# Pairs of column chunks of a feed-forward's first matrix multiplied as seven block products instead of eight, with the matrix pieces queued by due time and x kept in DRAM meanwhile

## The chip, the cores and the metric

The program runs on one core of one Trainium2 chip. The core's engines are TensorE (PE in the profile, with its weight loads as PEld), VectorE (DVE), ScalarE (ACT), GpSimd (POOL) and SyncE (SP), which here issues the DMAs. The metric is the device time of one execution in microseconds (us), the median of several runs; lower is better. Before the change it is 1352.48 us, the median of three runs (1351.2 to 1352.58).

## The reference

The model has two layers. Each is a feed-forward sub-layer, a token mixer and a second feed-forward sub-layer, on 256 tokens of 1024 channels in float32. The change touches only the four feed-forward sub-layers, and in them only the product with the first matrix:

```python
def swiglu_ffn(h, w_in, w_out):                 # w_in: 1024 x 5632, w_out: 2816 x 1024
    gate, up = jnp.split(h @ w_in, 2, axis=-1)
    return (jax.nn.silu(gate) * up) @ w_out

for i in range(DEPTH):                          # DEPTH = 2
    f = swiglu_ffn(rmsnorm(x, ffn1_norm_pre[i]), ffn1_w_in[i], ffn1_w_out[i])
    x = x + 0.5 * rmsnorm(f, ffn1_norm_post[i])
    ...                                         # the token mixer
    f = swiglu_ffn(rmsnorm(x, ffn2_norm_pre[i]), ffn2_w_in[i], ffn2_w_out[i])
    x = x + 0.5 * rmsnorm(f, ffn2_norm_post[i])
```

## The kernel before

**How a float32 product is made.** Every operand of a large product is split in two: a part `hi`, the value rounded to TensorE's one-pass float32 format (`F32R`), and a part `lo`, the value less `hi`. A product is three matmuls that add up in PSUM: hi by hi, hi by lo, lo by hi (`mm3`, L588). The activations are split once for each sub-layer, into `xt`. The matrices come from DRAM as pieces of 128 partitions x 1024 elements, 512 KB each, and each piece is split on the chip: ScalarE casts `whi<-raw` (128x1024), and then VectorE, or GpSimd in some places of the mixer, subtracts `wlo<-raw,whi`.

**The first product of a feed-forward.** `w_in` is laid out as 11 chunks of 512 columns, 256 of the gate and 256 of the matching up columns. One chunk is four pieces; each holds two blocks of 128 rows of the 1024 rows by the 512 columns. `proj_in` (L594) goes over the chunks. For each it multiplies both blocks of 128 tokens (`tb` 0 and 1) by every piece, 12 matmuls of 512 columns for a piece and 48 for a chunk, and `ev` turns the sums in PSUM into gated values: ScalarE takes Silu of the first 256 columns (`ag<-mm,rstd`), VectorE multiplies by the other 256 (`ag<-mm,rstd,ag`). `fin` transposes the gated values in small blocks on VectorE (`way<-ag`), sends them through DRAM to finish the transposition (the DMAs `way<-way`), and splits the outcome for the second product: ScalarE casts `act<-way`, GpSimd subtracts `act<-way,act` (128x512). The second product (`proj_out`, 22 pieces of `w_out`) reads `act`; `post` then adds to `x`.

**What sets the order.** PE executes in the order in which the program is written. The class `Stream` (L243) runs the pieces: `load` issues a piece's DMA and its two splitting instructions whenever PE is done with a piece. There are four buffers for `raw` and `RING = 8` for `whi` and for `wlo`, so splits can be at most eight pieces ahead of PE. In a feed-forward every `wlo` is on VectorE (the list `side` is False there). `Lanes` issues the smaller jobs (the transposed activations, the steps of `fin`) at counted ticks of PE's program. In the profile nearly all instructions stand at the lines of helpers: L144 and L150 for PE, L124 for VectorE and GpSimd, L171 for ScalarE, so they are told apart by the names of what they write and read.

## Time and profile before

| | |
|---|---|
| span of the profiled execution | 1349.7 us |
| median of the three runs | 1352.48 us |
| PE busy | 1327.1 us, 98% of the span |
| VectorE busy | 933.8 us, 69% |
| ScalarE busy | 732.3 us, 54% |
| GpSimd busy | 445.5 us, 33% |
| mean granted TensorE clock | 0.999 of full speed |

The profile is of one execution; its span, from the first to the last instruction, is 1349.7 us. What lies around the span is not in the profile: the median of the runs is 2.8 us more. Matmuls are pipelined, so the duration of one matmul in the profile is about twice the distance from one to the next, and "PE busy" is an upper bound. The share of an engine is a mean over stages that differ: in the chain of waits the long stretches of PE in the four feed-forwards begin at 14, 506, 688 and 1175 us and last 158 to 169 us each; the mixers lie between the first and the second, and between the third and the fourth. In an idle time, the name after the arrow is what ended it.

### The profile page before, as it was taken

The numbers are of one execution on the slowest core, as the hardware profiler recorded it, in microseconds if no ns is written. First come the engines' busy times: TensorE is split into PE (matmuls) and PEld (weight loads), VectorE is DVE, ScalarE is ACT, GpSimd is POOL, SyncE is SP. The second block draws the span as 40 slices with busy tenths as digits, with TensorE's granted clock in tenths as the row PEclk, the third lists the DMA queues.
The fourth block names the chain that finished last, engine by engine and source line by source line (L and its number), as shares of the span: only waits on it lengthen the run. The fifth ranks groups of instructions, "written<-read, shape, count | busy, mean of one in ns | idle before, by whom it ended". The sixth has DMA issues, their size and how long they took to land.

```text
span 1349.7 us, 20220 instructions
## 1 busy us (share of the span) xinstructions
PE 1327.1 (98%) x7259; PEld 1128.0 (84%) x7259; DVE 933.8 (69%) x1594; ACT 732.3 (54%) x1175; POOL 445.5 (33%) x374
## 2 busy tenths in 40 slices
PE   9999999999999999999999999999999999999998
PEld 7888889997787888888888888899977878888886
DVE  6676455999966776665576654579999666766553
ACT  7545447675555545544455543577656564555541
POOL 0111017798744201111011120277986431011110
PEclk9999999999999999999999999999999999999999
DMA  8878746562634666776468775465545446477861
GB/s 274 287 239 260 249 156 210 166 211 96 206 110 153 225 218 222 276 249 221 155 219 280 265 235 186 146 231 172 173 138 183 143 139 234 154 261 247 273 212 39
DMA packets 115652, 273.76 MB, mean 203 GB/s; under 512 B 24768, under 2 KB 48352, under 8 KB 115552
## 3 DMA queue, kind: packets, MB, share of 16 engines
q1 hardware_dynamic: 115264, 272.40, 61.5%
q8 instruction: 57, 0.93, 0.3%
q14 instruction: 43, 0.35, 0.1%
q10 hardware_dynamic: 288, 0.07, 0.0%
HBM read 256.68 MB, written 15.75 MB: 202 GB/s over the span
## 4 chain that ended last, share of the span: by engine, by line
PE 81%; DVE 11%; ACT 3%; DMA 2%; issue 1%; POOL 1%; DVEq 0%; POOLq 0%; SPq 0%; ACTq 0%
PE mm L144 75%; DVE cacc L124 4%; PE gd L144 3%; DVE c L124 3%; DVE wlo L124 2%; PE tr L150 2%; DMA raw<-mw 2%; ACT whi L171 1%; DVE at L124 1%; ACT dt L171 1%; ACT sg L171 0%; DMA raw<-w2i 0%; DVE ssk L124 0%; DVE qk L124 0%; POOL rk L124 0%
## 5 line engine op out<-in xcount | busy, mean ns | idle before, releaser
L144 PE MATMUL mm<-whi,xt 128*128 128x512 f32 (+1 forms) x2048 | 647.6, 391 | 3.0 <-ACT qT L171 2.2
L171 ACT CAST whi<-raw 128x1024 fp32r<-128x1024 f32 (+2 forms) x448 | 458.8, 1035 | 316.8 <-PE mm L144 173.8
L124 DVE TENSOR_TENSOR wlo<-raw,whi 128x1024 fp32r<-128x1024 f32 (+2 forms) x342 | 427.2, 1264 | 190.0 <-ACT whi L171 183.5
L144 PEld LDWEIGHTS mm<-whi,xt 128*128 128x128 f32 x2048 | 382.3, 188 | 82.3 <-ACT qT L171 3.0
L144 PE MATMUL mm<-wlo,xt 128*128 128x512 f32 (+1 forms) x1024 | 396.4, 387 | 0.1
L124 POOL TENSOR_TENSOR wlo<-raw,whi 128x1024 fp32r<-128x1024 f32 (+1 forms) x106 | 250.5, 2379 | 142.5 <-ACT whi L171 140.0
L144 PEld LDWEIGHTS mm<-wlo,xt 128*128 128x128 f32 x1024 | 192.6, 188 | 37.6 <-DVE wlo L124 1.3
L144 PE MATMUL mm<-whi,act 128*128 128x512 f32 x704 | 218.3, 390 | 0.0
L124 POOL TENSOR_TENSOR act<-way,act 128x512 fp32r<-128x512 f32 x44 | 79.1, 1798 | 396.1 <-ACT act L171 385.9
L124 DVE SCALAR_TENSOR_TENSOR cacc<-hT,pc,cacc 128x254 f32<-128x254 f32 (+28 forms) x464 | 179.5, 472 | 0.2
L144 PE MATMUL mm<-xt,whi 128*128 128x256 f32 x960 | 175.5, 285 | 0.8 <-ACT qT L171 0.6
L144 PEld LDWEIGHTS mm<-whi,act 128*128 128x128 f32 x704 | 132.2, 188 | 27.4
L144 PEld LDWEIGHTS mm<-xt,whi 128*128 128x128 f32 x960 | 149.4, 192 | 1.9 <-ACT qT L171 0.9
L144 PE MATMUL mm<-wlo,act 128*128 128x512 f32 x352 | 137.0, 389 | 0.0
L144 PE MATMUL mm<-xt,wlo 128*128 128x256 f32 x480 | 135.9, 283 | 0.0
L171 ACT ACTIVATE ag<-mm,rstd 128x256 f32<-128x256 f32 x88 | 41.7, 474 | 100.0 <-PE mm L144 80.5
L144 PEld LDWEIGHTS mm<-xt,wlo 128*128 128x128 f32 x480 | 92.0, 192 | 0.0
L124 DVE SCALAR_TENSOR_TENSOR ag<-mm,rstd,ag 128x256 f32<-128x256 f32 x88 | 42.3, 481 | 58.7 <-ACT ag L171 58.4
L144 PEld LDWEIGHTS mm<-wlo,act 128*128 128x128 f32 x352 | 66.1, 188 | 13.6
L124 POOL TENSOR_TENSOR rpost<-ss,exp 128x1 f32<-128x1 f32 x12 | 6.5, 538 | 193.8 <-DVE ss L124 193.8
L171 ACT ACTIVATE jk<-mm 128x512 f32<-128x512 f32 x24 | 14.3, 598 | 60.4 <-PE mm L144 60.4
L124 DVE SCALAR_TENSOR_TENSOR c<-mm,pc,c 128x255 f32<-128x255 f32 (+2 forms) x108 | 43.7, 478 | 2.6 <-ACT c L171 2.6
(187 smaller groups left out, 1148.3 us busy)
## 6 DMA issues: line engine op xcount, KB each, us to landing
raw<-mw SPq DMA_DIRECT2D x168, 512.0 KB, 3.8
raw<-w2i SPq DMA_DIRECT2D x88, 512.0 KB, 4.8
raw<-w1i SPq DMA_DIRECT2D x84, 512.0 KB, 4.9
raw<-w1o SPq DMA_DIRECT2D x44, 512.0 KB, 4.7
raw<-w2o SPq DMA_DIRECT2D x44, 512.0 KB, 4.3
way<-way SPq DMA_DIRECT2D x176, 64.0 KB, 1.8
way<-way SPq DMA_DIRECT2D x44, 256.0 KB, 4.8
wbc<-feat SPq DMA_DIRECT2D x13, 512.0 KB, 4.9
```

Of the source, the lines that this page charges most:

```text
L124: r = op(out, *a, **k)
L144: r = self.eng.matmul(o, w, x, **k)
L150: r = self.eng.transpose(*a)
L171: r = op(*a, **k)
```

## The change

Two consecutive chunks make a unit: the 1024 rows and the 1024 columns of the two chunks are seen as a matrix of 2 x 2 blocks of 512 rows and 512 columns, and the activations as 2 x 2 blocks of 128 tokens and 512 channels. The unit's product of two 2 x 2 block matrices is computed from seven block products instead of eight (the Winograd form of Strassen's algorithm). Chunks 6, 7 and 9, 10 of the first feed-forward and 3, 4, 6, 7 and 9, 10 of the other three are units, 11 in all; the other chunks stay as they were. The parts:

- `unit` does seven products of 12 matmuls, 84 where two chunks had 96. Three intermediate sums are copied from PSUM by ScalarE (`kept`), and three of the four results are finished by an addition on VectorE (`gate`, `ag<-mm,sm`, 128x512) ahead of Silu and the multiplication, both then on values in SBUF.
- A unit needs seven matrix forms of two pieces each: three blocks as they are (named 11, 21, 22) and four sums (t1 to t4). So 14 pieces are cast and subtracted where there were eight, and eight more 128x1024 subtractions make the sums, in place in the tiles that hold the raw pieces. Those tiles stay occupied longer; besides the four `raw` buffers they are free slots of the activations (`held`) and the two tiles of `x` (`x0`, `x1`).
- For this, `x` is written to DRAM when the sub-layer begins (`spill`; in the very first it is there already) and read back during the second product (`back`).
- `early` makes the four sums of activation blocks (`xs`) once for each sub-layer, on VectorE and ScalarE.
- From `early` to the end of the first product the pieces are no longer split as they come: `Stream.plan` and what it calls place casts, subtractions and sums on ScalarE, VectorE and GpSimd by planned times and by when PE needs each piece, `bring` issues the DMAs, and `in_order` fixes the order on the three engines as planned. GpSimd takes weight subtractions and sums there, and the subtraction `act<-way,act` moves from GpSimd to VectorE.

```diff
+UNITS = ({6: {"11": (8, 9), "12": ("x0", "x1"), "22": (7, 13), "21": (10, 17)},
+          9: {"11": (9, 10), "12": ("x0", "x1"), "21": (13, 17)}},) + 3 * (
+    {3: {"11": (5, 6), "12": (7, 8), "22": (9, None), "21": (10, 17)}, 6: {"11": (8, 9), "12": ("x0", "x1"), "22": (None, 13), "21": (10, 17)},
+     9: {"11": (9, 10), "12": ("x0", "x1"), "21": (13, 17)}},)
...
+FORMS = ("11", "t1", "t2", "21", "t3", "22", "t4")
+SUMS = {"t1": ("12", "12", "11"), "t2": ("12", "22", "12"), "t3": ("11", "12", "11"), "t4": ("21", "21", "12")}
...
 class Stream:
...
+    def bring(self, now):
+        while self.raws:
+            raw = self.raws[0]
...
+            if self.fetch > now + CFG["depth"]:
+                break
+            self.raws.pop(0)
+            raw.tile = self.fresh() if raw.key is None else self.held(raw.key)
+            self.nc.sync.dma_start(raw.tile[:, :raw.src.shape[-1]], raw.src)
...
+    def best(self, eng, now, until, ahead):
...
+        at, mine = max(eng.at, now), max(self.vec.at, now)
+        for p in self.pieces[self.taken:self.nload + ahead]:
+            kind, t = self.jobs(p)
+            dead = due
+            due += p.use
...
+            if eng is self.gp:
+                mine = max(mine, t) + 1.17
+                if t + 2.4 > max(mine, dead - (CFG["slack"] if kind == "low" else CFG["sums"])):
+                    continue
...
+    def issue(self, eng, t, p, kind):
...
+        if kind == "sum":
+            a, b = (r.tile for r in p.ins)
...
+                eng.tensor_tensor(p.raw.tile, a, b, op=ALU.subtract)
...
+        elif kind == "high":
+            self.to_high(p, slice(0, n))
...
+            self.to_low(p, slice(0, n), eng)
...
     def ffn(xt, l, units, wpost, after, first=2, tails=None):
...
-                    W.tensor_tensor(lo, src, hi.bitcast(F32), op=ALU.subtract)
+                        V.tensor_tensor(lo, src, hi.bitcast(F32), op=ALU.subtract)
...
+        def early():
...
+            def whole(o, r, h):
+                t = blk[r, h].bitcast(F32)
+                V.tensor_tensor(o, t[:, 0], t[:, 1], op=ALU.add)
...
+            def high(n, src):
+                S.copy(sums[n][:, 0], src)
...
+            def low(n, src):
+                V.tensor_tensor(sums[n][:, 1], src, sums[n].bitcast(F32)[:, 0], op=ALU.subtract)
...
+            for eng in (V, W, S):
+                eng.in_order(tc)
+            if spill is not None:
+                for tb in range(2):
+                    nc.sync.dma_start(spill[tb], x[tb])
+            st.plan(lanes)
+            sums["job"] = lanes.add("forms", steps())
...
+        def unit(c):
...
+                        mm3(ps, f[:, 0, kt, :], f[:, 1, kt, :], w[0][:, ks], w[1][:, ks], start and kt == 0, kt == 3,
+                            skip_group_check=True)
...
+                        V.tensor_tensor(a.rearrange("p a b -> p (a b)"), ps, more, op=ALU.add)
...
+                        S.activation(a[:, 0, :], a[:, 0, :], AF.Silu, scale=xt[tb][1])
...
+                        V.scalar_tensor_tensor(a[:, 1, :], a[:, 1, :], xt[tb][1], a[:, 0, :], op0=ALU.mult, op1=ALU.mult)
...
+            product(q, blk[0, 0], True)
+            kept(q, s1)
+            product(r, sums[1], True)
+            kept(r, s5)
+            product(q, sums[2], False)
+            kept(q, s2)
+            s = ps_mm()
+            product(s, blk[0, 1], True)
+            gate(c, 0, s, s1)
+            product(q, sums[3], False)
+            gate(c + 1, 1, q, s5)
+            product(r, sums[4], False)
+            gate(c + 1, 0, r, s2)
+            product(q, blk[1, 1], False)
+            gate(c, 1, q)
...
+        def back():
+            for tb in range(2):
+                x[tb] = xtile(tb)
+                nc.sync.dma_start(x[tb], x_in[tb * P:tb * P + P, :] if spill is None else spill[tb])
+                yield
```

The diff says little of where the instructions stand, since a planner places them. The first place is VectorE in the second feed-forward of the first layer, around chunk 6. Before, its rows there are splits of pieces (`wlo`), the gating of a chunk (`ag`) and its transposes (`way`):

```order
L124 SCALAR_TENSOR_TENSOR ag_5873<-mm_5788,rstd0_5096,ag_5873 128x256
L124 TENSOR_TENSOR wlo_5849<-raw_5847,whi_5848 128x1024
L124 SCALAR_TENSOR_TENSOR ag_5876<-mm_5789,rstd1_5215,ag_5876 128x256
L124 STREAM_TRANSPOSE way_5891<-ag_5873 128x2x4x32
L124 STREAM_TRANSPOSE way_5891<-ag_5876 128x2x4x32
L124 TENSOR_TENSOR wlo_5869<-raw_5867,whi_5868 128x1024
L124 TENSOR_TENSOR wlo_5905<-raw_5903,whi_5904 128x1024
```

After the change the same stretch reads so (`x0`, `x1` and `held` are tiles that hold raw pieces or their sums; a row that writes one of them is a sum):

```order
L139 TENSOR_TENSOR x0_5749<-x0_5749,held_5734 128x1024
L139 TENSOR_TENSOR x1_5764<-x1_5764,held_5736 128x1024
L139 TENSOR_TENSOR wlo_5787<-x1_5764,whi_5786 128x1024
L139 TENSOR_TENSOR x0_5749<-raw_5783,x0_5749 128x1024
L139 TENSOR_TENSOR x1_5764<-held_5805,x1_5764 128x1024
L139 SCALAR_TENSOR_TENSOR ag_5883<-mm_5792,rstd0_5160,ag_5883 128x256
L139 SCALAR_TENSOR_TENSOR ag_5885<-mm_5793,rstd1_5279,ag_5885 128x256
L139 TENSOR_TENSOR wlo_5823<-x0_5749,whi_5822 128x1024
L139 STREAM_TRANSPOSE way_5913<-ag_5883 128x2x4x32
L139 STREAM_TRANSPOSE way_5913<-ag_5885 128x2x4x32
L139 TENSOR_TENSOR wlo_5843<-x1_5764,whi_5842 128x1024
L139 TENSOR_TENSOR held_5736<-x1_5764,held_5736 128x1024
```

Five of the unit's sums now stand among the gating and the transposes of chunk 5, the plain chunk ahead of the unit, and the splits read the tiles that the sums wrote. For this unit and the plain chunk behind it VectorE has 16 instructions of 128x1024 (5 sums, 11 splits).

The second place is GpSimd in the same sub-layer. Before, it had nothing there but the small scales and the 11 subtractions of `fin`:

```order
L124 TENSOR_TENSOR rpost<-ss_5204,exp_80 128x1
L124 TENSOR_TENSOR rstd_5215<-ss,exp_80 128x1
L124 TENSOR_TENSOR act<-way,act 128x512 x11
L124 TENSOR_TENSOR rpost<-ss_6567,exp_80 128x1
L124 TENSOR_TENSOR rstd_6582<-ss,exp_80 128x1
```

After the change, for the unit of chunks 6 and 7 and the plain chunk 8, it has these ten:

```order
L139 TENSOR_TENSOR wlo_5758<-held_5736,whi_5757 128x1024
L139 TENSOR_TENSOR wlo_5773<-x0_5749,whi_5772 128x1024
L139 TENSOR_TENSOR held_5734<-x0_5749,held_5734 128x1024
L139 TENSOR_TENSOR wlo_5863<-held_5830,whi_5862 128x1024
L139 TENSOR_TENSOR wlo_5882<-held_5840,whi_5881 128x1024
L139 TENSOR_TENSOR held_5830<-held_5830,x0_5749 128x1024
L139 TENSOR_TENSOR held_5840<-held_5840,x1_5764 128x1024
L139 TENSOR_TENSOR wlo_5988<-raw_5856,whi_5987 128x1024
L139 TENSOR_TENSOR wlo_6000<-raw_5872,whi_5999 128x1024
L139 TENSOR_TENSOR wlo_6027<-raw_5985,whi_6026 128x1024
```

Seven of the unit's 22 instructions of 128x1024 and three of the plain chunk's four stand on GpSimd. In the whole sub-layer GpSimd has 32 of them where it had none, and 24 in the first sub-layer of the program; the `act` subtractions are gone from it.

More of the change, by code (lines that the diff above doesn't have):

```diff
@@ L216, in tick @@
         if self.stream is not None:
+            self.stream.act.at = max(self.stream.act.at, self.pe.at)
+        if self.stream is not None:
             self.stream.tick()
@@ L257, in __init__ @@
         self.lanes, self.his, self.lows, self.still = None, [], [], True
+        self.planned, self.begun, self.raws, self.out, self.fetch = False, 0.0, [], [], 0.0
     def load(self, count=1):
@@ L317, in in_step, with plan @@
         self.lanes = lanes
+    def plan(self, lanes):
+        if lanes is not None:
+            self.planned, self.lanes, lanes.stream, self.begun = True, lanes, self, self.pe.at
+            self.raws = []
+            for p in self.pieces[self.nload:self.nload + 120]:
+                for raw in p.group or [p.raw]:
+                    if raw not in self.raws:
+                        raw.first = p.n
+                        self.raws.append(raw)
+            self.out = []
+        else:
+            for p in self.pieces[self.taken:self.nload]:
+                self.force(p)
+            self.planned, self.lanes.stream, self.lanes = False, None, None
@@ new lines, in bring @@
+    def bring(self, now):
+        while self.raws:
+            raw = self.raws[0]
+            self.out = [r for r in self.out if not r.free(now)]
+            if raw.first > self.taken + RING + CFG["far"]:
+                break
+            if sum(r.key == raw.key for r in self.out) >= (4 if raw.key is None else 1):
+                break
+            if self.fetch > now + CFG["depth"]:
+                break
+            self.raws.pop(0)
+            raw.tile = self.fresh() if raw.key is None else self.held(raw.key)
+            self.nc.sync.dma_start(raw.tile[:, :raw.src.shape[-1]], raw.src)
+            self.fetch = max(self.fetch, now) + 1.9
+            raw.landed = self.fetch + CFG["land"]
+            self.out.append(raw)
@@ new lines, in jobs, with latest @@
+    def jobs(self, p):
+        def latest(times):
+            return None if any(t is None for t in times) else max(times, default=0.0)
+        if p.form in SUMS and p.summed is None:
+            t = latest([getattr(q, did) for q, did in p.needs] + [r.landed for r in p.ins])
+            return ("sum", t)
+        if p.hi is None:
+            return (None, None)
+        if p.high is None:
+            return ("high", p.summed if p.form in SUMS else p.raw.landed)
+        if p.low is None:
+            return ("low", p.high)
+        return (None, None)
@@ L319, in peek, with force @@
+    def force(self, p):
+        until = self.pe.at
+        while p.low is None:
+            until += 0.5
+            if until > self.pe.at + 100:
+                raise RuntimeError(f"stuck {p.n} {p.form}")
+            self.bring(until)
+            self.pump(until)
     def peek(self, i):
-        if self.lanes is not None:
+        if self.planned:
+            self.force(self.pieces[self.taken + i])
+        elif self.lanes is not None:
             self.tick(self.taken + i)
@@ L633, in proj_in @@
                 ev(c, 0, pss[c])
+        if first and early:
+            early()
         for c in range(len(chunks)):
+            if c in units:
+                unit(c)
+            if c in units or c - 1 in units:
+                continue
+            if c == 1 and not first and early:
+                lanes.finish(due[1])
+                early()
             if c in by_ch:
@@ new lines, in steps @@
+            def steps():
+                a = gated[c, tb] = tokt("ag", [P, 2, 256])
+                with prio(tc, "ev"):
+                    S.activation(a[:, 0, :], ps[:, 0:256], AF.Silu, scale=xt[tb][1])
+                yield
+                with prio(tc, "ev"):
+                    V.scalar_tensor_tensor(a[:, 1, :], ps[:, 256:512], xt[tb][1], a[:, 0, :], op0=ALU.mult, op1=ALU.mult)
+            job = lanes.add("gate", steps())
+            if st.planned:
+                lanes.step(job)
+            else:
+                lanes.finish(job)
@@ L733, in lhs @@
+        proj_in(xt, [(512, 2)] * 11, ev, fin_one, first, units=units, unit=unit, early=early)
+        st.plan(None)
+        lanes.flush()
+        for eng in (V, W, S):
+            eng.in_order(None)
+        wbc = load_feat(l, wpost, 17)
+        def back():
+            for tb in range(2):
+                x[tb] = xtile(tb)
+                nc.sync.dma_start(x[tb], x_in[tb * P:tb * P + P, :] if spill is None else spill[tb])
+                yield
+        lanes.add("back", back())
         def lhs(kt, tb):
```

295 lines of the change are left out of this document (228 added, 67 removed), and 1 row of the table DELAY.

## The prediction

> **What bounds the kernel now.** I read the page first, then the chain of waits in order of time.
>
> ```profile
> span 1349.7 us, 20220 instructions
> PE 1327.1 (98%) x7259; PEld 1128.0 (84%) x7259; DVE 933.8 (69%) x1594; ACT 732.3 (54%) x1175; POOL 445.5 (33%) x374
> PE 81%; DVE 11%; ACT 3%; DMA 2%; issue 1%; POOL 1%; DVEq 0%; POOLq 0%; SPq 0%; ACTq 0%
> ...
> 13.63 163.60 PE mm L144 x720
> 506.41 164.68 PE mm L144 x726
> 687.97 157.90 PE mm L144 x696
> 1174.69 168.77 PE mm L144 x744
> ```
>
> The last four lines are the four feed-forwards: PE alone, without a wait, for some 160 us each. A matmul of 512 columns costs 164.68 / 726 = 0.227 us there, a piece (12 matmuls) 2.72 us. So the change works on stages where PE is the whole bound, and each matmul taken away is worth 0.227 us as long as the other engines keep up. How much room they have is told by the windows (columns: length, then PE, PEld, DVE, ACT, POOL busy, clock, DMA share, GB/s):
>
> ```profile
> 506.00:671.00 165.00, 165.00 (x731) 136.47 (x730) 98.62 (x112) 81.30 (x101) 21.28 (x13) 1.00 0.67 222
> 204.00:488.00 284.00, 276.57 (x1912) 246.30 (x1912) 227.64 (x510) 172.04 (x328) 174.59 (x151) 1.00 0.53 173
> ```
>
> In a feed-forward (first row) VectorE is busy 60% and GpSimd 13%. In the mixer (second row) both work hard at once. The groups by form give the prices:
>
> ```profile
> L171 ACT CAST whi<-raw 128x1024 fp32r<-128x1024 f32 x432 | 449.0, 1049 | 310.3 <-PE mm L144 170.9 <-DMA raw<-mw 55.0 <-DMA raw<-w1i 27.3
> L124 DVE TENSOR_TENSOR wlo<-raw,whi 128x1024 fp32r<-128x1024 f32 x332 | 420.6, 1281 | 179.0 <-ACT whi L171 172.5
> L124 POOL TENSOR_TENSOR wlo<-raw,whi 128x1024 fp32r<-128x1024 f32 x100 | 242.4, 2440 | 128.7 <-ACT whi L171 126.2 <-DVE cacc L124 1.7 <-PE tr L150 0.2
> L124 POOL TENSOR_TENSOR act<-way,act 128x512 fp32r<-128x512 f32 x44 | 79.1, 1798 | 396.1 <-ACT act L171 385.9 <-DMA raw<-w2i 10.2
> L124 DVE SCALAR_TENSOR_TENSOR ag<-mm,rstd,ag 128x256 f32<-128x256 f32 x88 | 42.3, 481 | 58.7 <-ACT ag L171 58.4
> L171 ACT ACTIVATE ag<-mm,rstd 128x256 f32<-128x256 f32 x88 | 41.7, 474 | 100.0 <-PE mm L144 80.5 <-issue 9.5 <-DVE ag L124 7.3
> L124 DVE STREAM_TRANSPOSE way<-ag 128x256 f32<-128x256 f32 x88 | 37.7, 438 | 3.2
> L171 ACT CAST act<-way 128x512 fp32r<-128x512 f32 x44 | 27.1, 616 | 2.7 <-DMA way<-way 2.7
> L171 ACT ACTIVATE jk<-mm 128x512 f32<-128x512 f32 x24 | 14.3, 598 | 60.4 <-PE mm L144 60.4
> L124 DVE TENSOR_TENSOR yb<-mm,wbc 128x512 f32<-128x512 f32 x8 | 5.5, 690 | 1.9 <-PE mm L144 1.5
> L124 DVE TENSOR_TENSOR wlo<-raw,whi 128x512 fp32r<-128x512 f32 x8 | 5.3, 687 | 3.9 <-ACT whi L171 3.9
> ```
>
> The means of the two `wlo` groups hide what decides here. A 128x512 subtraction takes GpSimd 1.80 us, though a 128x1024 one takes 2.44. The timeline shows why. First VectorE and GpSimd at 357 us, in the mixer, then both at 744 us, in a feed-forward:
>
> ```profile
> 356.86 2.26 DVE L124 SCALAR_TENSOR_TENSOR cacc<-hT,pc,cacc 128x228 f32<-128x228 f32 x6
> 359.02 1.96 DVE L124 TENSOR_TENSOR wlo<-raw,whi 128x1024 fp32r<-128x1024 f32 x1
> 357.50 5.73 POOL L124 TENSOR_TENSOR wlo<-raw,whi 128x1024 fp32r<-128x1024 f32 x2
> ...
> 744.03 4.60 DVE L124 TENSOR_TENSOR wlo<-raw,whi 128x1024 fp32r<-128x1024 f32 x3
> 745.59 1.95 POOL L124 TENSOR_TENSOR act<-way,act 128x512 fp32r<-128x512 f32 x1 [9.89 <-ACT act L171]
> ...
> 310.81 1.13 DVE wlo L124
> ...
> L124 DVE TENSOR_TENSOR wlo<-raw,whi x342: 679/1225/2311, 5.2 to 1322.8; 128x1024 fp32r<-128x1024 f32 x166, 128x512 fp32r<-128x512 f32 x4, 128x544 fp32r<-128x544 f32 x1
> L124 POOL TENSOR_TENSOR wlo<-raw,whi x106: 1358/2404/3416, 192.1 to 1133.4; 128x1024 fp32r<-128x1024 f32 x100, 128x544 fp32r<-128x544 f32 x6
> ```
>
> The last two rows give min/median/max: 1.225 us is normal for VectorE, 2.404 us for GpSimd. In the chain of waits, where the next instruction starts before the shown end, a split on VectorE counts 1.13 (the row above them), so I take 0.09 off the other durations of VectorE too. At 357.50 GpSimd's first split runs to 359.90. VectorE's split begins at 359.02 and ends at 360.98, 1.08 us after GpSimd's end instead of 1.225 us after its own start. GpSimd's second split ends at 363.23, 2.25 us after VectorE's. **They take turns**: one pair costs 1.08 + 2.25 = 3.33 us, as if on one engine. At 744 us three splits of VectorE need 4.60 us where 3 x 1.13 = 3.39 would do; the 1.21 us more is a 128x512 instruction of GpSimd in between. The six `cacc` rows are not held up, though GpSimd starts its split under them: 2.26 / 6 = 0.38 us each. They read one operand from SBUF and the other from PSUM. So I count every instruction of VectorE with two large SBUF operands, and every one of GpSimd, on one common lane, and the rest of VectorE beside it.
>
> [...]
>
> **The change part by part.** Removed: 12 matmuls in each of 11 units, 132 x 0.227 = 30.0 us of PE, if nothing else waits. Put against it, for a unit and a plain chunk behind it (where the order shows it: chunks 6 to 8):
>
> - PE: 132 matmuls, 29.96 us; before, 144 and 32.69.
> - ScalarE: 18 casts at 1.05, six Silu at 0.47, three `act` casts at 0.62, three copies from PSUM priced by `jk<-mm` at 0.60: 25.4 us. It fits under 30, at 85%, so 0.
> - The common lane: 10 instructions on GpSimd and 16 on VectorE of 128x1024. Ten pairs at 3.33 and six alone at 1.13 are 40.1; three `act` subtractions, now VectorE's, at 0.60 (row `wlo` 128x512) and three in-place gatings at 0.39 add 3.0: **43.1 us**.
>
> So the lane needs 43 us where PE needs 30. A ring of eight pieces and sums done ahead move this about but can't supply it, so I sum over the whole stretch from the planner's start to the last split of the third unit. PE: the second halves of chunks 0 and 1, three plain chunks, three units: 444 x 0.227 = 100.8 us; before, 480 and 109.0. Lane: 30 on GpSimd x 2.25 = 67.5; of 48 on VectorE 30 at 1.08 and 18 at 1.13, 52.7; eight `act` and nine early activation sums x 0.60 = 10.2; eight gatings x 0.39 = 3.1: **133.5 us**, 24.5 above the 109.0 of before. To it comes what VectorE does that needs neither the lane nor GpSimd's pause: 18 transposes x 0.35, nine additions out of PSUM x 0.60 (row `yb`), nine gatings x 0.39, 15.2 us. While GpSimd has work these lie under its turns, and it has for 30 x 3.33 = 100 of the 134 us; I take a third, 5 us (0 to 15.2). The first pieces of the planned stretch:
>
> ```profile
> raw<-w2i SPq DMA_DIRECT2D x88, 512.0 KB, 4.8
> ```
>
> Twelve pieces and two spills of `x` come in before the first unit; at 222 GB/s a piece is 2.4 us, so the lane starves a little at first: 1.5 us (0 to 8). Sum: 24.5 + 5 + 1.5 = 31 us for each of three sub-layers, 93 us.
>
> The first sub-layer has two units, late: 22 on GpSimd and 43 on VectorE make 49.5 + 47.5, with 12.2 of small ones 109.2 us, against 109.0 of PE before; with a third of the free work 4 us (0 to 12).
>
> At nothing: spill and `back` of `x`, 14 transfers of 2.4 us. The DMA share is 0.67 and the pieces are as many as before over a longer stretch; `x` is needed only after the 22 pieces of the second product, 60 us later. If this cover is gone, at most 2 x 2.4 us a sub-layer. The second product has one split per 2.72 us and no GpSimd work, so it neither stalls nor gives anything back. The copies out of PSUM have one product (2.72 us) until the bank is written again and take 0.6.
>
> Total 93 + 4 = 97 us. The span becomes 1349.7 + 97 = 1447; the median was 2.8 above the span, so I predict **1450 us**. Its own range: 24.5 x 3 = 74 with everything else hidden (1426), and (24.5 + 15.2 + 8) x 3 + 12 = 155 with all of it exposed (1508).
>
> **The rivals.** A, *faster*: VectorE and GpSimd work side by side. Then a cycle has 24.4 us on GpSimd (10 x 2.44) and about 18 + 8 on VectorE (16 x 1.13 and the small ones) against 30 of PE; all is hidden, 30 us are gained and perhaps 4 lost at edges: 1326 us. For it speaks the mixer's window, where 228 and 175 us of both fit in 284; against it that VectorE's work there is mostly on PSUM operands, and the turns above, to a hundredth of a microsecond. It decides where fewer than about four of a cycle's splits on GpSimd meet one of VectorE.
>
> B, *the lane is real but light*: only the full-size pairs that the trace shows take turns; activation sums, `act` and gatings do not, and free work is hidden. 67.5 + 52.7 = 120.2, 11.2 above before, times three, less 5.5 (24 matmuls) in the first sub-layer, where PE would still be the bound: 1352.5 + 28 = 1380 us.
>
> C, *worse than the lane*: the three orders are fixed, so a VectorE addition that waits for a late product holds the splits behind it, and GpSimd those of VectorE that need its sums; or PE's clock falls in the gaps. In
>
> ```profile
> 204.00:216.00 12.00, 10.83 (x57) 8.96 (x57) 3.51 (x4) 8.80 (x14) 8.48 (x5) 1.00 0.66 222
> ```
>
> PE idles 1.17 us of 12 and the clock stays 1.00; gaps of a turn, 3.33 us, the trace doesn't have. At half rate a unit takes 19.1 us more, of which the lane's 13.1 (43.1 less 29.96) cover most: 6.0 x 11 = 66 us, 1516 us and up. [...]
>
> **How the numbers follow.** Forecast 0.74, A 0.08, B 0.08, C 0.10. Two in ten left out are A, half of B and most of C: 1390 to 1520 us. A measurement of this kernel tells about 0.2% (2.7 us) from no change. Slower: forecast, C and nearly all of B, 0.91; within 0.2% takes 0.01 of B; faster is A, 0.08.
>
> **What would show it.** PE's share in the windows of the feed-forwards falls to some 75%, with waits of PE for `wlo` of VectorE and GpSimd; the medians of `wlo` there rise to about 2 us on VectorE and 3.3 us on GpSimd; from the first planned split to the last of a unit triple 135 to 145 us pass, the second products keep 0.227 us a matmul, and the clock stays at 1.00. I am wrong if VectorE's splits stay at 1.2 us while GpSimd's run beside them, or if PE waits mostly for ScalarE or DMA.

## The result and the profile after

The changed kernel takes 1540.91 us (median of four runs, 1540.24 to 1543.49) beside 1351.84 us for the kernel before on the same chip: a ratio of 1.1402, 95% interval 1.1386 to 1.1418. It is 189 us slower, where 1450 us, 97 us slower, was forecast. The first lines of its page:

```profile
span 1538.5 us, 20196 instructions
PE 1373.6 (89%) x7127; PEld 1141.6 (74%) x7127; DVE 1232.6 (80%) x1753; ACT 816.2 (53%) x1290; POOL 723.7 (47%) x450
PEclk9988999999999998979998988999999999979889
PE 42%; DVE 35%; issue 9%; ACT 7%; DMA 5%; POOL 2%; DVEq 0%; POOLq 0%; ACTq 0%; SPq 0%
```

The 132 matmuls are gone (7259 before, 7127 now), but PE's share of the chain of waits fell from 81% to 42% and VectorE's rose from 11% to 35%. I take as a feed-forward's first product the time from the last matmul of the stage ahead of it (or the start) to the first matmul that reads `act`, and as the second the time from there to the last matmul that reads it:

| us, before / after | FF1 | FF2 | FF3 | FF4 |
|---|---|---|---|---|
| first product | 128.1 / 154.2 | 121.1 / 169.5 | 121.1 / 169.4 | 121.7 / 169.0 |
| second product | 60.8 / 64.8 | 60.5 / 64.9 | 60.9 / 66.1 | 60.0 / 64.3 |

First products lose 26 + 48 + 48 + 47 us, second products 4.0 to 5.2 us each. The mixers lose 1 us together. The windows (columns as before) show the planned stretch of the second feed-forward, then the two halves of the first feed-forward's planned stretch, before and within its units:

```profile
538.00:685.00 147.00, 112.83 (x427) 87.18 (x425) 141.74 (x110) 71.96 (x94) 92.91 (x32) 0.88 0.43 145
17.00:80.00 63.00, 62.77 (x273) 50.77 (x273) 52.47 (x61) 37.27 (x50) 27.67 (x11) 1.00 0.78 260
80.00:144.00 64.00, 49.76 (x185) 38.11 (x183) 62.66 (x49) 35.29 (x46) 43.54 (x14) 0.87 0.48 155
```

VectorE has an instruction open in 141.74 of 147 us (a wait for its turn counts as busy). In the first feed-forward PE is hardly idle up to 80 us, and idle 14 of 64 us after. The groups by form, as in the prediction:

```profile
L139 DVE TENSOR_TENSOR wlo<-held,whi 128x1024 fp32r<-128x1024 f32 x70 | 155.6, 2238 | 4.3 <-ACT whi L194 4.3
L139 POOL TENSOR_TENSOR wlo<-held,whi 128x1024 fp32r<-128x1024 f32 x38 | 117.6, 3105 | 60.0 <-ACT whi L194 57.2 <-DMA held<-w1i 1.7 <-DMA held<-w2i 1.1
L139 POOL TENSOR_TENSOR held<-held,x 128x1024 f32<-128x1024 f32 x14 | 46.7, 3355 | 0.2
L139 DVE TENSOR_TENSOR act<-way,act 128x512 fp32r<-128x512 f32 x44 | 53.3, 1227 | 4.0 <-ACT act L194 3.9
```

A split that takes VectorE 1.225 us alone lasts 2.24 us on average in its group here, one of GpSimd 3.11 in place of 2.40. The other kinds that the prediction put on the lane take turns as well: begun beside a running GpSimd instruction, an `act` subtraction lasts 2.8 or 2.9 us in place of 0.68, an activation sum (`xs`) 2.5 to 2.9 in place of 0.68, an in-place gating 1.3 to 2.6 in place of 0.47. The timeline around 620 us shows the turns, VectorE first, then GpSimd:

```profile
619.82 3.41 DVE L139 TENSOR_TENSOR held<-x,held 128x1024 f32<-128x1024 f32 x1
623.15 3.39 DVE L139 TENSOR_TENSOR wlo<-held,whi 128x1024 fp32r<-128x1024 f32 x1
626.46 3.41 DVE L139 TENSOR_TENSOR wlo<-raw,whi 128x1024 fp32r<-128x1024 f32 x1
629.79 3.42 DVE L139 TENSOR_TENSOR act<-way,act 128x512 fp32r<-128x512 f32 x2
...
615.43 6.71 POOL L139 TENSOR_TENSOR wlo<-held,whi 128x1024 fp32r<-128x1024 f32 x2
622.11 6.68 POOL L139 TENSOR_TENSOR held<-held,x 128x1024 f32<-128x1024 f32 x2
628.80 3.27 POOL L139 TENSOR_TENSOR wlo<-raw,whi 128x1024 fp32r<-128x1024 f32 x1
```

Each turn of the pair is 3.3 us long, from one start to the next, on both engines. Of the waits in that feed-forward's first product, those of PE and of ScalarE's casts (us in total, times, longest):

```profile
PE mm L159 <- DVE wlo L139: 20.6, 9, 6.2
ACT whi L194 <- DVE x L139: 20.1, 5, 8.2
ACT whi L194 <- DVE held L139: 20.0, 4, 8.3
PE mm L159 <- ACT sm L194: 11.2, 2, 8.3
```

PE waits for VectorE's splits; behind the row `ACT sm` stands VectorE again, since ScalarE's copy is queued behind casts that wait up to 8.3 us for VectorE's sums. The second product's loss is one place in VectorE's queue (VectorE, then PE):

```profile
694.13 4.89 DVE L139 TENSOR_TENSOR wlo<-raw,whi 128x1024 fp32r<-128x1024 f32 x4 [0.26 <-ACT whi L194]
698.94 0.47 DVE L139 SCALAR_TENSOR_TENSOR ag<-mm,rstd,ag 128x256 f32<-128x256 f32 x1
...
699.56 0.47 PE L159 MATMUL mm<-whi,act 128*128 128x512 f32 x1 [2.51 <-DVE ag L139]
```

The last chunk's gating, which frees a PSUM bank that PE needs, stands behind four splits of the second matrix; PE waits 2.51 us and then runs at half clock (0.50) for 3.4 us.

### The profile page after: what moved, and what is told of

Same layout as the page of the kernel before. It is cut to its first block, busy times and chain, and to the rows that moved or that the text cites. A ratio compares the mean times of both kernels' runs of the same rounds, so it can differ in the third digit from the quotient of the medians.

```text
span 1538.5 us, 20196 instructions
## 1 busy us (share of the span) xinstructions
PE 1373.6 (89%) x7127; PEld 1141.6 (74%) x7127; DVE 1232.6 (80%) x1753; ACT 816.2 (53%) x1290; POOL 723.7 (47%) x450
## 4 chain that ended last, share of the span: by engine, by line
PE 42%; DVE 35%; issue 9%; ACT 7%; DMA 5%; POOL 2%; DVEq 0%; POOLq 0%; ACTq 0%; SPq 0%
PE mm L159 37%; DVE wlo L139 13%; ACT whi L194 4%; DVE x L139 3%; PE gd L159 3%; DVE ag L139 3%; DVE cacc L139 3%; DVE held L139 3%; DVE act L139 3%; DVE c L139 2%; DMA raw<-w1i 2%; PE tr L165 2%; DVE way L139 1%; POOL wlo L139 1%; DMA raw<-mw 1%
## 5 line engine op out<-in xcount | busy, mean ns | idle before, releaser
L159 PE MATMUL mm<-whi,xt 128*128 128x512 f32 (+1 forms) x1608 | 531.6, 402 | 22.0 <-DVE ag L139 18.9
L194 ACT CAST whi<-raw 128x1024 fp32r<-128x1024 f32 (+2 forms) x374 | 379.8, 1031 | 238.0 <-PE mm L159 132.0
L139 POOL TENSOR_TENSOR wlo<-raw,whi 128x1024 fp32r<-128x1024 f32 (+1 forms) x146 | 359.9, 2479 | 233.7 <-ACT whi L194 216.1
L139 DVE TENSOR_TENSOR wlo<-raw,whi 128x1024 fp32r<-128x1024 f32 (+1 forms) x228 | 306.1, 1358 | 113.9 <-ACT whi L194 109.6
L159 PE MATMUL mm<-whi,xs 128*128 128x512 f32 x352 | 136.2, 459 | 44.6 <-ACT sm L194 40.4
L139 DVE TENSOR_TENSOR wlo<-held,whi 128x1024 fp32r<-128x1024 f32 x70 | 155.6, 2238 | 4.3 <-ACT whi L194 4.3
L139 POOL TENSOR_TENSOR wlo<-held,whi 128x1024 fp32r<-128x1024 f32 x38 | 117.6, 3105 | 60.0 <-ACT whi L194 57.2
L194 ACT CAST whi<-held 128x1024 fp32r<-128x1024 f32 x108 | 109.7, 1046 | 61.1 <-DVE held L139 60.0
L159 PE MATMUL mm<-wlo,xs 128*128 128x512 f32 x176 | 85.4, 485 | 57.7 <-DVE wlo L139 54.5
L159 PEld LDWEIGHTS mm<-whi,xs 128*128 128x128 f32 x352 | 79.9, 227 | 66.6 <-ACT sm L194 43.8
```

The costliest lines, as they stand in the source:

```text
L139: r = op(out, *a, **k)
L159: r = self.eng.matmul(o, w, x, **k)
L194: r = op(out, *a, **k)
```

## The experiments

The expectations call the prediction's theory *lane*: VectorE's instructions with two SBUF operands and all of GpSimd's take turns, and their work sets the stretch. Against it stand *half clock*, *side by side*, and *ring* (waits at the head of fixed queues). Ratios are to the kernel before on the same chip (1350.82 to 1352.45 us), with 95% intervals.

**1. One operand from PSUM.** Only VectorE's planned sums and splits are altered:

```diff
-            eng.tensor_tensor(p.lo[:, c], p.raw.tile[:, c], p.hi.bitcast(F32)[:, c], op=ALU.subtract)
+            if self.planned and eng is self.vec:
+                eng.tensor_tensor(p.lo[:, c], p.hi.bitcast(F32)[:, c], self.junk.broadcast_to([P, c.stop - c.start]), op=ALU.subtract)
...
+                    eng.tensor_tensor(p.raw.tile, p.chain.tile, self.junk.broadcast_to([P, D]), op=ALU.subtract)
```

> The changed kernel, but each planned split and sum on VectorE reads one of its operands from PSUM (a bank of zeros, one column of it broadcast) in place of SBUF; engine, order, size, buffers and nearly all waits stay, and GpSimd keeps its share. It leaves out the true second operand, so what it computes in the feed-forwards is not the reference's. Lane: with one SBUF operand the instructions stop taking turns with GpSimd's, the 3.3 us pairs come apart, TensorE bounds the first products again and the time falls to between 1322 and 1380. Fixed orders (waits at the head of three engines' queues set the time, whatever one instruction lasts): the order is the same, so the time stays above 1480. Half clock: falls only if the gaps of TensorE go.

Measured 1400.22 us, 1.0359 (1.0331 to 1.0387): 141 of the 189 us go, with the same plan. The window of the stretch:

```profile
513.00:622.00 109.00, 98.88 (x427) 79.09 (x425) 100.40 (x111) 72.08 (x96) 77.30 (x32) 1.00 0.60 204
```

And its timeline, VectorE and then GpSimd:

```profile
577.50 2.34 DVE L139 TENSOR_TENSOR wlo<-whi,junk 128x1024 fp32r<-128x1024 f32 x2
579.92 4.67 DVE L139 TENSOR_TENSOR act<-way,act 128x512 fp32r<-128x512 f32 x2
...
574.08 4.79 POOL L139 TENSOR_TENSOR wlo<-held,whi 128x1024 fp32r<-128x1024 f32 x2
578.84 5.20 POOL L139 TENSOR_TENSOR held<-held,x 128x1024 f32<-128x1024 f32 x2
```

The same 32 instructions of GpSimd now take 77.3 us, and VectorE's altered 128x1024 instructions 1.17 to 1.22 us each, beside GpSimd's or not. The two `act<-way,act` subtractions, which still read two SBUF operands, last 4.67 us in place of some 1.3: in one kernel, within 3 us, an instruction is held or not by where its second operand lies. The edit also drops some waits: a split no longer reads the raw piece, and a sum reads one piece where it read two. But an instruction's own duration holds no such wait, and VectorE's busy time falls by 41 us for 111 instructions in place of 110, while the stretch falls by 38. So the turns are shown, as cause of 141 us with all that follows from them. The time is above the 1322 to 1380 expected: 48 us have another cause.

**2. TensorE kept warm.** Four spare matmuls before each of a unit's 14 steps:

```diff
+                    for _ in range(4):
+                        nc.tensor.matmul(spare, idle[:, 0:P], idle[:, P:640], start=True, stop=True)
```

> The changed kernel with four spare matmuls (128x512, into a bank that nobody reads) ahead of each of a unit's 14 steps: 616 more matmuls, 140 us of TensorE at 0.227 us, all placed where TensorE waits in the changed kernel (13 us a cycle idle against 12.7 us added). Nothing that the reference asks for is left out. Half clock: the gaps shrink, the clock stays at 1.00, and the time falls below 1480. Lane: TensorE is not what the stretch waits for; the clock may rise but the time stays within 20 us of 1541.

Measured 1540.37 us, 1.1389 (1.1358 to 1.1419), with the clock at 0.982 over the span in place of 0.944. The same stretch:

```profile
539.00:686.00 147.00, 137.22 (x581) 93.90 (x588) 140.16 (x111) 72.89 (x96) 95.56 (x32) 0.98 0.45 151
```

PE is busy 24 us longer, the clock is back at 0.98, and the stretch still lasts 147 us. This run alone can't tell much: with the spare matmuls PE has 612 x 0.227 = 139 us of work in the stretch, so no more than 8 us of the 147 could have gone, in three feed-forwards less than half of the 60 us that *half clock* asked for. What bounds the cost of the half clock is the lane: one of its instructions is open during 136.6 of the 146.7 us in the changed kernel, and 136.7 of 146.1 here. So in a later first product at most some 10 us of the stretch can be due to it.

**3. No units, all else.** `UNITS = 4 * ({},)`.

> The changed kernel with the planner by due times, the store and the return of x and the subtraction of the second product's input on VectorE, but with no seven-product units: every pair of chunks is computed with eight block products as before. Nothing is left out of the computation. Lane: without the units' sums and extra splits the lane has about 36 us less than in the changed kernel in each stretch, TensorE bounds the first products, and the time is the one before within 10 us (1342 to 1362). Rival: the new queues by due time or x's way through DRAM cost by themselves, 1370 or more.

Measured 1362.17 us, 1.0072 (1.0044 to 1.0100). This is the upper end of what lane expected. In the profiled execution first products are within 2 us of before, and most of the difference lies in the second products (62.2, 64.9, 63.2 and 61.5 us). The units bring nearly all of the loss, the planner with all else some 10 us of it.

**4. GpSimd taken out.**

```diff
-            can = [(found, k) for k, eng in enumerate((self.act, self.vec, self.gp))
+            can = [(found, k) for k, eng in enumerate((self.act, self.vec))
```

> The changed kernel, but its planner hands weight work only to ScalarE and VectorE; GpSimd gets no full-size split, sum or difference in the feed-forwards. Everything computed stays. Three theories of the 189 us that the change lost. Lane (the prediction's own): VectorE's instructions with two SBUF operands and GpSimd's take turns at 3.3 to 3.4 us, so moving GpSimd's share to VectorE makes the pair cheaper (2 x 1.08 to 1.13 us in place of 3.33). In a stretch from the start of the planner to the last matmul of a first product (146.7 us in the changed kernel) VectorE would then have about 78 such instructions, 88 us, and some 30 us of other work, 119 us in all; about 27 us less in each of three feed-forwards, about 20 less in the first: some 1430 us. Side by side (the prediction's first rival): GpSimd was help, and without it the time rises above 1541. Half clock alone: the time falls only as far as TensorE's gaps shrink; if the clock stays as low as in the changed kernel (0.94 over the span), the time stays above 1500.

Measured 1610.28 us, 1.1914 (1.1885 to 1.1944): slower, which lane did not expect. The number is what *side by side* expected, but its reason is not: VectorE is not short of GpSimd's help, it idles. The window of the stretch:

```profile
541.00:702.00 161.00, 122.58 (x427) 89.47 (x425) 117.39 (x140) 72.14 (x95) 0.98 (x1) 0.86 0.40 130
```

One chain in its timeline (VectorE, ScalarE, PE):

```profile
628.99 0.69 DVE L139 TENSOR_TENSOR ag<-mm,sm 128x512 f32<-128x512 f32 x1 [1.51 <-PE mm L159]
629.60 2.35 DVE L139 TENSOR_TENSOR held<-x,held 128x1024 f32<-128x1024 f32 x2
631.98 1.23 DVE L139 TENSOR_TENSOR wlo<-held,whi 128x1024 fp32r<-128x1024 f32 x1
...
630.90 2.18 ACT L194 CAST whi<-held 128x1024 fp32r<-128x1024 f32 x2 [3.39 <-DVE held L139]
...
632.00 0.79 PE L159 MATMUL mm<-whi,xs 128*128 128x512 f32 x1 [3.05 <-ACT whi L194]
633.26 0.79 PE L159 MATMUL mm<-wlo,xs 128*128 128x512 f32 x1 [0.47 <-DVE wlo L139]
```

VectorE has the 117 us that lane gave it (119 forecast) and idles 44 us. It waits for PE's product to add it, then makes the next product's sums, ScalarE casts them, VectorE splits, and PE waits through all of it: a ring.

**5. Work laid out further ahead.** `beat=0.68` becomes 6, in the changed kernel, in the one without GpSimd, and in the one of experiment 1:

> The changed kernel with one number of the planner altered: it lays out work up to 6 us ahead of TensorE in place of 0.68, so that casts, sums and subtractions stand ahead of the additions that wait for a product's end. Same amount of work, nearly the same shares (11 rows move from GpSimd to VectorE). Lane (work that takes turns fills the stretch): of the 146.7 us of a stretch 135 are work of the lane, so at most 12 us can go in each of the feed-forwards: 1495 to 1545. Ring (waits in the fixed orders set the time): the time falls below 1450.

> The kernel without GpSimd (1610 us) with the planner laying out work up to 6 us ahead of TensorE in place of 0.68. Everything is computed. Here nothing takes turns, and VectorE alone has about 119 us of work in a stretch that lasts some 160. Ring: the waits go, the stretch comes near VectorE's 119 us, and the time falls to 1400 to 1480. If it stays above 1580, the order of the queues within these 6 us is not what makes that kernel slow.

> The kernel whose planned VectorE instructions read one operand from PSUM (1400 us) with the planner laying out work up to 6 us ahead. It leaves out the true second operand as that one did. Lane and ring together: with neither turns nor an order just in time, TensorE bounds the first products, and some 9 us in each of three feed-forwards go: 1365 to 1375, or lower if the units' 30 us come out whole (1340). Rival: the 48 us that are left over the kernel before lie elsewhere (the start of the second products, 4.5 us each), and the time stays within 10 us of 1400.

Measured 1537.92 (1.1384, 1.1365 to 1.1403), 1596.82 (1.1819, 1.1798 to 1.1840) and 1380.95 us (1.0221, 1.0206 to 1.0236). The changed kernel does not answer. Without GpSimd the time stays above 1580, so by the sign given the order within these 6 us is not what makes it slow. With a PSUM operand the time lies between the two expectations: the three later first products come down to 121 us, as before the change, but not below it, while the first one rises from 127.7 to 138.0 us.

**6. Ahead of VectorE's own backlog.** A planned VectorE that is late gets no more work, so the plan falls back to one piece at a time. Hence:

```diff
-        until = now + CFG["beat"] if until is None else until
+        until = max(now, self.vec.at) + CFG["beat"] if until is None else until
```

(`beat` is 3 here.)

> The changed kernel, whose planner lays out work up to 3 us beyond the later of TensorE's and VectorE's planned times, in place of 0.68 us beyond TensorE's alone. With 6 us beyond TensorE nothing changed (1538 us), and the reason may be that VectorE's planned time is then far ahead of TensorE's, so that the planner lays out each piece only when TensorE asks for it, behind the addition that waits for the product before. Here sums and subtractions stand ahead of these additions as far as buffers allow. Same work, 13 rows fewer on GpSimd. Lane: 135 us of work that takes turns remain in a stretch of 146.7, so the time is 1490 to 1541. Ring of waits: below 1450.

> The kernel without GpSimd (1610 us) with the same rule: work laid out up to 3 us beyond the later of TensorE's and VectorE's planned times. Everything is computed. Ring: the waits in VectorE's queue go, and VectorE's own work sets the stretch, 78 instructions of 128x1024 at 1.13 us and some 30 us of others, 119 us; 10 us over the kernel before in three feed-forwards, and 10 us in each of the four second products as that kernel has them: 1400 to 1450. That would make GpSimd's share in the changed kernel a loss of about 100 us. If it stays above 1560, VectorE's order is not the cause.

Measured 1581.97 us (1.1699, 1.1679 to 1.1718) with GpSimd, worse than the changed kernel, and 1501.06 us (1.1105, 1.1084 to 1.1126) without, 109 us better than 1610. Both lie outside what was expected. Without GpSimd order is a large part of the loss; with it, this order is worse: the lane is open 141 us of stretches of 157 to 159 us.

**7. A plan that knows what happens.** One line lets planned TensorE wait for a late piece; in the changed kernel two more let planned VectorE and GpSimd take turns:

```diff
+        self.pe.at = max(self.pe.at, p.low)
...
+        if kind != "high":
+            self.vec.at, self.gp.at = max(self.vec.at, eng.at), max(self.gp.at, eng.at)
```

> The changed kernel, whose planner now counts that sums and subtractions on VectorE and GpSimd take turns, and that TensorE waits when a piece is late. The units are the same, and GpSimd has 239 instructions of 128x1024 in place of 228 in the whole program, so the work that takes turns is as much as before; only its order answers to the turns. Lane: that work sets the stretch, 1500 to 1560. Order: if the loss came from an order laid out for engines side by side, the time falls below 1450.

> The kernel without GpSimd (1610 us) with the line by which planned TensorE waits for a late piece. Everything is computed. Plan theory: the order again follows what the engines can do, the waits of the ring go, and VectorE's 119 us set the stretch: 1420 to 1500, as with work laid out beyond VectorE's planned time (1501) or better. If the ring is the units' own, above 1560.

Measured 1583.58 us (1.1710, 1.1690 to 1.1729), above both expectations, and 1482.76 us (1.0971, 1.0955 to 1.0988), within the plan theory's. The window of the stretch with GpSimd:

```profile
544.00:703.00 159.00, 115.41 (x426) 87.75 (x424) 140.91 (x111) 76.71 (x98) 101.75 (x36) 0.84 0.43 144
```

And without:

```profile
533.00:663.00 130.00, 110.78 (x426) 85.53 (x425) 119.63 (x142) 76.84 (x99) 0.84 (x1) 0.91 0.51 170
```

Without GpSimd VectorE is busy 119.6 of 130 us: its own work is now most of the bound. The later first products are still 23 to 26 us longer than before, and the second products 9 to 12 us, each with one long wait for the last gating. With GpSimd no order tried (1538, 1582, 1584) beats the one given by more than 3 us. In the order given GpSimd's share helped (1610 us without it); of the best orders that were run, it is a loss: 1538 us with it, 1483 without.

**8. One unit, and the start of the second product.** One unit per feed-forward, no GpSimd; then the same with no more than two pieces of the second matrix laid out before the last gating, and with the multiplication of chunk 10's gating issued right behind its Silu; then the same lines in the changed kernel.

```diff
+            if p.tail >= 2 and not self.ending:
+                break
...
-            if st.planned:
+            if st.planned and c < 10:
                 lanes.step(job)
```

> One unit (chunks 6 and 7) in each feed-forward and no weight work on GpSimd there; everything is computed. 48 matmuls fewer than in the kernel before, 10.9 us of TensorE. The kernel with the planner and no unit took 1362.17 us. Load theory: over the stretch VectorE has about 84 us of work in 106 us, so it keeps up and the time is about 1362 less 11, 1345 to 1355. Ring theory (formed after the run without GpSimd came out slower, 1610 us, with VectorE busy only two thirds of the time: a product's end, the addition on VectorE, the next sum, the cast on ScalarE and the subtraction on VectorE follow one after another while TensorE waits): inside the unit VectorE has 22 instructions of 128x1024, 25 us, against 19 us of TensorE, so it falls behind, the same chain forms there, and the time is over 1362.

> The kernel with one unit in each feed-forward and no GpSimd (1393.68 us; first products 121 us in the later three, as before, but second products 68 to 71 us in place of 61, each with one gap of 5.6 to 7.9 us on TensorE that VectorE's gating of the last chunk ends). Here the planner lays out no more than two pieces of the second matrix before that gating. Everything is computed. If the gating stood behind splits of the second matrix (the queue's order), the second products return to 61 or 62 us and the time is 1360 to 1367. If they were late for another reason, it stays at 1394.

> The changed kernel with one rule more: the planner lays out no more than two pieces of the second matrix before the gating of the last chunk. Everything is computed. In the kernel with one unit this rule gave 36 us back and brought the second products to 60 or 61 us. Queue order alone: here too they fall from 64 to 66 us to 61, 17 us, and the time is about 1524. Lane behind it: VectorE is so far behind its plan at the end of a first product that the gating is late whatever stands ahead of it; then the second products stay at 64 us or more and the time within 6 us of 1541.

One unit: 1393.68 us (1.0313, 1.0298 to 1.0329). That is above 1362, as the ring theory had it, but for another reason: nearly all of the loss is in the second products, 68 to 71 us. ScalarE, VectorE and PE there:

```profile
633.37 1.04 ACT L192 CAST whi<-raw 128x1024 fp32r<-128x1024 f32 x1 [1.58 <-DMA raw<-w2o]
634.32 0.83 ACT L192 ACTIVATE ag<-mm,rstd 128x256 f32<-128x256 f32 x2
...
638.13 0.87 DVE L137 SCALAR_TENSOR_TENSOR ag<-mm,rstd,ag 128x256 f32<-128x256 f32 x2
...
638.76 0.77 PE L157 MATMUL mm<-whi,act 128*128 128x512 f32 x1 [6.56 <-DVE ag L137]
```

The last Silu stands behind a cast that waits for its DMA, the gating behind splits, and PE waits 6.56 us. With the rule the second products are 60.8, 60.5, 60.9 and 60.0 us, as before the change to a tenth, and the time is 1357.72 us (1.0037, 1.0026 to 1.0048): 36 us for the order of one place. In the changed kernel the same lines make it worse, 1560.61 us (1.1547, 1.1531 to 1.1562), with second products of 71 us, and neither number that I had written for it was right. The timeline shows why (VectorE, then PE):

```profile
700.93 1.23 DVE L139 TENSOR_TENSOR wlo<-raw,whi 128x1024 fp32r<-128x1024 f32 x1 [3.23 <-ACT whi L194]
702.82 5.00 DVE L139 TENSOR_TENSOR wlo<-raw,whi 128x1024 fp32r<-128x1024 f32 x3 [0.67 <-ACT whi L194]
708.78 1.23 DVE L139 TENSOR_TENSOR wlo<-raw,whi 128x1024 fp32r<-128x1024 f32 x1 [0.96 <-ACT whi L194]
709.93 0.47 DVE L139 SCALAR_TENSOR_TENSOR ag<-mm,rstd,ag 128x256 f32<-128x256 f32 x1
...
710.55 0.77 PE L159 MATMUL mm<-whi,act 128*128 128x512 f32 x1 [7.66 <-DVE ag L139]
```

Here chunks 9 and 10 are one unit, and its last gating carries the number 9. So `c < 10` lets its multiplication come later as before, and the splits that were held back are laid out ahead of it, five of them. The order that was meant was therefore not tried in the changed kernel.

A further run put these lines into the kernel without GpSimd of experiment 6. Expected were 30 to 40 us less than its 1501.06 us, 1370 to 1415; measured were 1501.63 us (1.1099, 1.1071 to 1.1127), with second products of 71 to 74 us. The reason is the same: six splits stand ahead of the last gating, and PE waits 8.79 us for it. What the rule would give in these two kernels stays open.

**9. Units with room around them, without GpSimd and with the rule of 8.** Chunks 3, 4 and 8, 9 in the three later feed-forwards; the same with the line of 7 on planned TensorE; and one unit in those three alone.

> Two units (chunks 3 and 4, and 8 and 9) in each of the three later feed-forwards, none in the first, three plain chunks between them, no weight work on GpSimd, and the rule for the second matrix. Everything is computed. Load theory: a unit and three plain chunks have 34 instructions of 128x1024 on VectorE, 38 us, and some 10 us of small ones, against 52 us of TensorE, so VectorE keeps up over the group; 72 matmuls fewer are 16.3 us: 1352 less 16 and 2 us for the planner in the first feed-forward, 1338. If a single unit (25 us of VectorE against 19 of TensorE) already makes TensorE wait, since eight pieces of lead are only 11 us when a piece of a unit is used in 1.36 us, the gain is eaten: 1350 to 1365.

> The kernel with two spaced units in three feed-forwards (1475 us), with one line more: when TensorE asks for a piece that is not planned yet, the planner moves TensorE's planned time to the end of that piece's split. Before, planned TensorE never waited, so that after a unit the planner laid out each piece only when it was asked for. Everything is computed. Plan theory: the chain of waits does not outlive a unit, and VectorE's 48 us of work in 52 us of TensorE fit: 1345 to 1380. Burst theory: the waits inside a unit come from the unit's own chain (addition, sum, cast, subtraction) and stay: above 1420.

> One unit (chunks 6 and 7) in each of the three later feed-forwards and none in the first, no weight work on GpSimd, and the rule for the second matrix. Everything is computed. The kernel with a unit in the first as well took 1357.72 us, 6.5 us more than the kernel before in the first feed-forward and 2 us less in the other three. Without that unit the first is as in the kernel without units (2 us more): 1353, no difference from before. Load theory without gaps: 36 matmuls, 8 us: 1346.

Measured 1475.34 us (1.0908, 1.0890 to 1.0927), 1397.00 us (1.0339, 1.0313 to 1.0365) and 1357.05 us (1.0035, 1.0022 to 1.0047); none lies where it was expected. The ring outlives the unit where the plan doesn't know of it (78 us), but even with a plan that does, two spaced units cost 12 to 18 us in each first product. The window of the second feed-forward's first product with two units and that plan:

```profile
501.00:637.00 136.00, 123.98 (x515) 98.30 (x514) 116.39 (x148) 74.06 (x100) 2.06 (x3) 0.96 0.62 208
```

And with one unit, in the kernel with the rule of 8:

```profile
500.00:621.00 121.00, 118.37 (x524) 96.95 (x524) 98.46 (x131) 66.75 (x92) 2.06 (x3) 1.00 0.71 237
```

VectorE is busy 116 of 136 us over the group, so the average would fit. It is the unit itself, with 22 of VectorE's instructions (25 us) against 19 us of PE, that makes PE wait: of PE's 12 us of idle time in the first window some 11 lie within the two units. With one unit PE stands idle 2.6 us of 121, just what 12 matmuls save. In the last kernel the first feed-forward has no unit at all, and its first product still takes 134.1 us, 6 more than before the change, while the three later feed-forwards together take 1.5 us less. So the 5 us that this kernel loses are not the unit's; they come with the planner as it is set here. Why it costs more there than in experiment 3 (130.0 us, with GpSimd) was not taken apart. No kernel that was run beats the one before.

## Why the prediction was wrong

- **Common lane: right.** In the three later stretches, from the first activation sum that VectorE writes to SBUF to the last matmul that reads such a sum, the time in which an instruction of the lane is open (VectorE's with two SBUF operands, in-place gatings included, and any of GpSimd) adds up in the trace to 136.6, 136.3 and 136.6 us, against 133.5 forecast. Turns of 3.3 us, PE's share (112.83 of 147, 77%), its waits for VectorE: all as said. The medians of the splits are 2.16 us on VectorE and 2.8 on GpSimd, where 2 and 3.3 were forecast, and from the first planned split to the last of the third unit 140 us pass, within the 135 to 145. That `act` subtractions, activation sums and in-place gatings stand on the lane (10.2 + 3.1 of the 133.5 us) was the prediction's estimate: no run before the change shows it, since none of them stands on VectorE there with two SBUF operands. In the changed kernel they take turns, 2.8 or 2.9, 2.5 to 2.9 and 1.3 to 2.6 us each when begun beside a running GpSimd instruction. Experiment 1 shows the cause.
- **The step that failed** is "24.5 + 5 + 1.5 = 31 us for each of three sub-layers". It let the lane run nearly without a pause. Measured are 48 us. The stretch lasts 146.7, 145.3 and 146.7 us, so the lane itself idles some 10 us in it while its next instructions wait, mostly for ScalarE's casts or PE's products; the terms for this, 6.5 us together, were too small, and the upper end of 23 held it. The rest, some 11 us, lies outside the stretch, above all at its end: PE's last product there waits 3.17 us for VectorE's addition (`ag<-mm,sm`) and then runs at half clock (0.50) for 4.58 us. Three times 17 us are a little over half of the miss.
- **The first sub-layer, 4 us: measured 26.** I spread its lane work over the whole stretch, where it equals PE's. The units lie behind some 75 us, and PE's window from 17 to 80 us, 62.77 of 63, shows that the room ahead of them went unused; behind 80 us VectorE is busy 62.66 of 64.
- **"Neither stalls nor gives anything back"**: the second products lost 4.0 to 5.2 us each. I had looked at the amount of work there, not at what stands ahead of the last gating: four splits, for which PE waits 2.51 us in the second feed-forward.
- **"The clock stays at 1.00"**: it fell to 0.88 in the stretch. By the lane's 136.6 of 146.7 us it can cost no more than some 10 us there.
- **Rivals.** A (side by side) falls with experiment 1. B (light lane) falls with the 136 us, and with the `act` subtractions, activation sums and gatings, which do take turns. C named 1516 us and up, where the time came out; but its half clock is not what sets the stretch, and its queues are only in part what happened: in the changed kernel four other orders gained 3 us or lost 20 to 43, while without GpSimd order alone was worth 128.
- **The median over the span**, 2.8 us forecast, was 2.4.

Open: of the 48 us that experiment 1 leaves, 19 are the second products and 29 the three later first products. In the first product of the second feed-forward there, PE idles 12.9 us, all of it within the units and 3.41 of it ahead of the last product, which waits for VectorE's addition; what each of these waits costs was not tested. Whether some order of the same work lets the lane run without its 10 us of pauses was not found, nor what the changed kernel takes with its last gating ahead of the second matrix.

## What to carry to other kernels

Count bursts as well as sums: in experiment 9 the average load of a stretch fits (VectorE busy 116 of 136 us), and TensorE still idles 12 us in it, some 11 of them within the two units, in each of which 25 us of VectorE's instructions stand against 19 us of TensorE's. Two engines that take turns (3.3 us for a pair here) are one engine in the plan, and handing work to the slower of them can cost more than it takes off the other: 1538 us with GpSimd against 1483 without, each in the best order that was run. Where orders are fixed by a plan, look for what stands ahead of the instruction that frees TensorE's next bank (36 us in the kernel with one unit, experiment 8), and check in the timeline that a new rule really moved it. Letting the plan's TensorE wait when the real one does was worth 128 and 78 us without GpSimd; together with planned turns it lost 43 us with GpSimd.

## What the runs showed of the hardware

- An operand in PSUM in place of SBUF takes VectorE's 128x1024 subtraction off the turns: 1.2 us beside a running GpSimd instruction (experiment 1), against turns of 3.3 us in the changed kernel. There VectorE's transposes (0.40 to 0.44 us) and its additions out of PSUM (0.68 us) are not held up by GpSimd either.
- In the changed kernel's trace TensorE's clock falls to half (0.50) 28 times: 9 times for 3.41 us, 13 times for 6.83, 5 times for 10.24, and once across the end of the span. Of TensorE's gaps with no other of 0.5 us or more within 12 us before and 7 us after, the one of 3.04 us, which ends at 84.03 us, is followed by a half of 3.41 us from 85.51 us on; in those of 5.03, 7.28, 8.22 and 8.27 us a half of 6.83 or 10.24 us begins; behind those of 1.03 to 1.72 us, seven here and six in the kernel before, the clock stays at 1.00. Behind the 2.51 us above, which are not alone (3.17 us lie 8 us ahead of them), a half of 3.41 us follows:

```profile
700.00:710.00 10.00, 10.00 (x39) 8.11 (x38) 4.42 (x6) 4.15 (x4) 0.00 (x0) 0.83 0.92 320
```
